# Column halves of w2, early norm weights and spread combining at the end of each layer's experts

## The chip, the cores and the metric

The kernel runs on one core of one Trainium2 chip. The metric is the time of one execution on the device in microseconds (us); several runs are taken and their median is compared. A profile of one execution gives the trace from which all rows below come. The engines are PE (matrix products), DVE and ACT (element-wise work), POOL, and SP, whose queue issues nearly all transfers.

## The reference

Two decoder layers and a closing norm over 512 tokens of width 1024, in float32. Layer 0 mixes tokens by forgetting attention, layer 1 by causal pooling over windows; behind each comes a mixture of 32 experts, of which every token takes two. Cut to what matters here:

```python
for i in range(DEPTH):
    h = modulate(rmsnorm(x, norm_mix_g[i]), sh_m, sc_m)
    y = fox_attention(...) if i % 2 == 0 else pool_mixer(...)
    x = x + gt_m * y
    h = modulate(rmsnorm(x, norm_ffn_g[i]), sh_f, sc_f)
    y = grouped_moe(h, ...)      # sum over chosen experts of w * (silu(h@w1) * (h@w3)) @ w2
    x = x + gt_f * y
return rmsnorm(x, norm_final_g)  # x * rsqrt(mean(x*x) + eps) * g
```

w1 and w3 are 1024 x 512 for each expert, w2 is 512 x 1024. All of them are read once from device memory: 32 experts, 6 MB each, in either layer.

## The kernel before, in words

The tokens lie in `xs` as four row blocks of 128 (t = 0 to 3), 1024 columns each. A layer's experts are worked off in 14 passes (`PASSES`); a pass takes one, two or four experts together. The last pass of each layer holds the four experts on places 8 to 11, each with at most 32 tokens, so that the products of the four stand side by side on 32 of 128 rows each (`parts`, with shares = 4).

**Weights.** `Stream` keeps a list of pieces of 1 MB in the order of use and 16 slots for them. `pump` issues the next piece on SP's queue whenever a slot is free; `done` frees a slot, with the last matmul that reads it. A pass of four experts has 8 pieces of w1, 8 of w3 and 8 of w2. A w2 piece (`expert_src`) is one half of the 512 inner rows with all 1024 columns: partition p holds the rows 4p to 4p+3, and half a of them (j = 2a, 2a+1) makes up a piece, 8 KB in one run for each partition. The pieces come in the order a = 0 of the four experts, then a = 1 of the four.

**A pass** (`step`, inside `experts`) multiplies the gathered tokens by w1 and w3 (`up`), gates them (`gated`), turns the result by transposes (`turn`) and multiplies by w2. In all passes but a layer's last, `down` fills two banks of 512 columns and the combining of a pass is done inside the next one. In a layer's last pass nothing follows, so it is written differently: `down_half` makes columns 0 to 511 first, `add_rows` spreads them over the four row blocks and adds them to `xs`, ACT takes the squares of that half for the norm (`half_length`), and then `down_half` makes columns 512 to 1023. Each half reads j = 0 to 3, so it needs all eight pieces; both are freed after the second half.

**After it** (`rows_step`) the second half is combined, square lengths are completed, and the norm's factor comes out. The order on PE, DVE, ACT and POOL is that of a hand-written string: `ORDER1` up to the bar for layer 0, `ORDER2` for layer 1. Its letters: K combines a row block on PE into a bank of tag c, T adds it to `xs` on DVE, Q takes the squares and R the root on ACT, N inverts on DVE. For layer 0, S is a small sum on PE, C scales `modC` on DVE by what S left, D scales the window matrix on DVE, and I multiplies by it on PE: with I the pooling layer begins. After `ORDER2` each row block of 1024 columns is multiplied by its factor and by the final norm weights in one DVE instruction (L1499) and sent out (L1500).

**Banks.** A tag of the PSUM pool has two banks. `add_rows` in the last pass and K use tag c alone for four row blocks, so that the third waits until the first has been added.

Of the kernel before, what the change touches and what calls it, by code (L numbers as in the profile page):

```python
# [24 lines left out]
D = 1024  # L25
T = 512
NT = 4
# [25 lines left out]
)  # L53
ORDER1 = (
# [9 lines left out]
)  # L64
ORDER2 = (
    "K0 K1 T0 Q0 R0 K2 T1 Q1 R1 N0 T2 K3 Q2 R2 N1 T3 Q3 R3 N2 N3 "
)


# [4 lines left out]
class Stream:  # L74
# [39 lines left out]
    def done(self, *keys):  # L114
        for key in keys:
            self.free[self.live.pop(key)[1]] += 1
        self.pump()
# [3 lines left out]
def kernel(  # L121
# [38 lines left out]
        stream.add(("wo", hf, a), attn_w_o[0].rearrange("(j p) n -> p j n", p=128)[  # L160
            :, 4 * a:4 * a + 4, 512 * hf:512 * hf + 512])

    def expert_src(w, l, k, a):

        static = k >= NE - STATIC
        e = k - (NE - STATIC) if static else order[l](k)
        v = w[l, e:e + 1] if static else w[l, ds(e, 1)]
        v = v.rearrange("o (p j) f -> p (o j) f", p=128)
        n = v.shape[1] // 2
        return v[:, n * a:n * a + n, :]  # L170

    def expert_items(l, i):

        for name, w in (("w1", exp_w1), ("w3", exp_w3), ("w2", exp_w2)):
            for a in range(2):
                for ab, k in enumerate(PASSES[i]):
                    stream.add((name, l, i, ab, a), partial(expert_src, w, l, k, a), lambda k=k: k >= NE - STATIC or l in order)

    order = {}

# [990 lines left out]
    def down_half(R, gT, gs, wt, hf, shares, done):  # L1171
        py = bank("y")
        for j in range(4):
            for r, ab in parts(shares):
                PE.matmul(py[r, :], gT[:, j, r], wt("w2", ab, j, hf), start=j == 0, stop=j == 3)  # L1175
        if hf:
            done("w2", 0)
            done("w2", 1)
        return weighted(R, gs, py, hf)

    def add_rows(PT, y, t, hf, tag="c"):
# [15 lines left out]
    def experts(R, aside):  # L1197
        l = R["l"]

        def weights(i):  # L1200
            def get(name, ab, j, hf):
                if hf is None:
                    return stream.get((name, l, i, ab, j // 4))[:, 512 * (j % 4):512 * (j % 4) + 512]
                at = 1024 * (j % 2) + 512 * hf
                return stream.get((name, l, i, ab, j // 2))[:, at:at + 512]

            def done(name, a):
                stream.done(*[(name, l, i, ab, a) for ab in range(len(PASSES[i]))])
            return get, done
# [22 lines left out]
        def step(i, xT, PT, gs, old, last):  # L1232

            w, done = weights(i)
            n = len(PASSES[i])
            p1, p3 = bank("h"), bank("h")
            if not last:
                Pn = choose(i + 1)
            if old:
                combine(old[0], old[1][0], 0, "cctt")  # L1240
            up(xT, w, "w1", p1, None if i else closing, n, done, (2, 6))
            if old:
                combine(old[0], old[1][1], 1, "ttyy")
            if not last:
                xg = gather(R, Pn)
            elif last == "layer":
                aside()
            up(xT, w, "w3", p3, None if i else closing, n, done, (2, 4, 6))
            g = gated(p1, p3)
            if not last:  # L1250
                xT = xgT()
                modulated(R, xg, xT)
            gT = turn(g)
            now = PT, gs
            if not last:
                PT, gs = chosen(i + 1, Pn)
            if last != "layer":
                return xT, PT, gs, (now[0], down(R, gT, now[1], w, n, done))
            y = down_half(R, gT, gs, w, 0, n, done)
            for t in range(NT):  # L1260
                add_rows(PT, y, t, 0)
                half_length(t, 0, mr("P16", [512], BF16))
                first_half(t)
            warm(AF.Sqrt, pre[:, NT - 1:])
            return PT, down_half(R, gT, gs, w, 1, n, done)

# [123 lines left out]
    def rows_step(PT, y, order):  # L1390
# [1 line left out]
        pa = {}  # L1392

        def K(t):
            ps = pa[t] = bank("c")
            PE.matmul(ps, PT[:, t, :], y[0], start=True, stop=False)
            PE.matmul(ps, PT[:, t, :], y[1], start=False, stop=True)

# [7 lines left out]
            root(t, pre[:, t:t + 1])  # L1406

        do = {"S": sums, "C": shift}
        for t in range(NT):
            for f in (K, T, Q, R):  # L1410
                do[f"{f.__name__}{t}"] = partial(f, t)
            do[f"N{t}"], do[f"D{t}"] = partial(inverse, t), partial(scaled, V, t)
            do[f"G{t}"] = partial(scaled, G, t)
# [75 lines left out]
    def gain():  # L1489
        last["fg"] = xgT().rearrange("p j t -> p (j t)")  # L1490
        G.dma_start(last["fg"], raw(norm_final_g, 0, [[0, 128], [1, D]]))

    end = experts(R, gain)
    with tc.manual_schedule(engines=BY_HAND):
        rows_step(*end, ORDER2)
    os = every([NT, 8, 128])
    for t in range(NT):
        o = os[:, t].rearrange("p j n -> p (j n)")
        V.scalar_tensor_tensor(o, xs[:, t, :], rstd[:, t:t + 1], last["fg"], op0=OP.mult, op1=OP.mult)  # L1499
        nc.sync.dma_start(out[0, 128 * t:128 * t + 128, :], o)  # L1500
    estack.close()


# [21 lines left out]
```

## Time and profile before

| | before |
|---|---|
| time, median of 3 runs | 1419.49 us (1413.96 to 1426.26) |
| the profiled execution's own time | 1410.96 us |
| its span, first to last instruction | 1409.4 us |
| PE busy | 1272.6 us, 90% of the span |
| DVE busy | 669.2 us, 47% |
| ACT busy | 384.6 us, 27% |
| mean granted TensorE clock | 0.967 of full |
| moved by transfers | 479.29 MB, 340 GB/s over the span |

A page of the profile cuts the span into 40 slices and gives in tenths how busy each engine was. In this one PE stands at 9 in most slices, the transfers too, with 410 to 421 GB/s in the stretches of experts; one slice between the two layers shows 74 GB/s, and the last slice 109 GB/s with PE at 4 tenths. A busy PE is not a PE at its peak, since its matmuls overlap; a wait shows in the timeline as idle time before an instruction, with what ended it.

### The profile page before, as it was taken

The numbers are of one execution on the slowest core, as the hardware profiler recorded it, in microseconds if no ns is written. First come the engines' busy times: TensorE is split into PE (matmuls) and PEld (weight loads), VectorE is DVE, ScalarE is ACT, GpSimd is POOL, SyncE is SP. The second block draws the span as 40 slices with busy tenths as digits, with TensorE's granted clock in tenths as the row PEclk, the third lists the DMA queues.
The fourth block names the chain that finished last, engine by engine and source line by source line (L and its number), as shares of the span: only waits on it lengthen the run. The fifth ranks groups of instructions, "written<-read, shape, count | busy, mean of one in ns | idle before, by whom it ended". The sixth has DMA issues, their size and how long they took to land. (4 is left out here: it accounts for less than half of the span.)

```text
span 1409.4 us, 18785 instructions
## 1 busy us (share of the span) xinstructions
PE 1272.6 (90%) x6688; PEld 665.7 (47%) x6689; DVE 669.2 (47%) x1306; ACT 384.6 (27%) x770; POOL 135.0 (10%) x90
## 2 busy tenths in 40 slices
PE   5789999888899699999999978899799999999984
PEld 2467777666443244444444425644244445444521
DVE  3787787885733233333334335743324334333423
ACT  3545555544421021111112104721021111111202
POOL 1513323425000000000000100100000000000000
PEclk9799999999999899999999997999999999999997
DMA  9654664756799999997999999289999998999992
GB/s 342 212 208 157 237 221 156 269 191 258 316 381 394 418 415 419 420 412 256 420 420 419 414 420 421 74 320 392 421 409 419 420 420 326 420 420 419 421 420 109
DMA packets 85000, 479.29 MB, mean 340 GB/s; under 512 B 12470, under 2 KB 25910, under 8 KB 29572
## 3 DMA queue, kind: packets, MB, share of 16 engines
q1 hardware_dynamic: 83776, 475.33, 84.2%
q10 hardware_dynamic: 496, 1.81, 0.4%
q8 instruction: 56, 0.92, 0.3%
q0 software_dynamic: 624, 0.84, 0.2%
q14 instruction: 48, 0.39, 0.1%
HBM read 475.55 MB, written 2.38 MB: 339 GB/s over the span
## 5 line engine op out<-in xcount | busy, mean ns | idle before, releaser
L1135 PE MATMUL h<-w,xgT 128*64 128x512 f32 (+2 forms) x2048 | 400.6, 595 | 1.3 <-ACT xgT L1070 0.6
L1135 PEld LDWEIGHTS h<-w,xgT 128*64 128x64 f32 (+2 forms) x2048 | 128.4, 130 | 237.4 <-issue 226.8
L1166 PE MATMUL y<-w,gT 128*64 128x512 f32 (+2 forms) x896 | 193.1, 596 | 16.7 <-DMA w<-in_exp_w_dram 9.9
L1187 DVE TENSOR_TENSOR xs<-xs,t 128x512 f32<-128x512 f32 x104 | 66.6, 682 | 144.0 <-PE t L1186 144.0
L1166 PEld LDWEIGHTS y<-w,gT 128*64 128x64 f32 (+2 forms) x896 | 60.4, 133 | 129.0 <-issue 99.8
L1156 DVE SCALAR_TENSOR_TENSOR y<-y,gs,gt 128x512 f32<-128x512 f32 x56 | 42.3, 755 | 162.4 <-PE y L1166 124.6
L701 POOL TENSOR_TENSOR wl<-w,wh 128x1024 fp32r<-128x1024 f32 x32 | 98.2, 3072 | 185.3 <-ACT wh L700 181.4
L1070 ACT ACTIVATE xgT<-t,modT 128x128 f32<-128x128 f32 x112 | 49.7, 458 | 206.7 <-PE t L1092 205.6
L1143 DVE TENSOR_TENSOR yl<-yl,h 128x512 f32<-128x512 f32 x28 | 19.3, 688 | 180.9 <-PE h L1135 161.6
L1126 ACT CAST yh<-y 128x512 fp32r<-128x512 f32 x56 | 32.9, 587 | 255.7 <-DVE y L1156 255.7
L301 DVE SCALAR_TENSOR_TENSOR lo<-w,cc,lo 128x2048 f32<-128x2048 f32 x28 | 82.1, 2931 | 0.4
L586 PE MATMUL c<-x,P 128*128 128x512 f32 x208 | 65.1, 436 | 9.0 <-DVE P L1101 9.0
L1141 ACT ACTIVATE yl<-h 128x512 f32<-128x512 f32 x28 | 16.8, 599 | 196.4 <-PE h L1135 196.4
L691 PE MATMUL h<-hi,wh 128*128 128x512 f32 x168 | 70.2, 418 | 0.0
L691 PE MATMUL h<-lo,wh 128*128 128x512 f32 x168 | 66.5, 396 | 0.0
L691 PE MATMUL h<-hi,wl 128*128 128x512 f32 x168 | 66.5, 396 | 0.0
L1075 DVE TENSOR_SCALAR yh<-c 128x512 f32<-128x512 f32 x26 | 18.0, 692 | 89.9 <-PE c L586 89.9
L586 PE MATMUL c<-lo,P 128*128 128x512 f16 x208 | 56.0, 393 | 0.0
L814 ACT ACTIVATE sb<-y,mx 128x128 f32<-128x128 f32 (+3 forms) x64 | 33.8, 528 | 75.7 <-DVE mx L813 73.4
L586 PEld LDWEIGHTS c<-x,P 128*128 128x128 f32 x208 | 40.4, 197 | 23.9 <-issue 12.0
L1127 DVE TENSOR_TENSOR yl<-y,yh 128x512 fp32r<-128x512 f32 x56 | 38.5, 688 | 21.1 <-ACT yh L1126 21.1
L1068 DVE TENSOR_SCALAR xgT<-t,modT 128x128 f32<-128x128 f32 x112 | 43.1, 406 | 9.2 <-ACT xgT L1070 8.5
(357 smaller groups left out, 1790.9 us busy)
## 6 DMA issues: line engine op xcount, KB each, us to landing
w<-in_exp_w_dram SPq DMA_DIRECT2D x384, 1024.0 KB, 17.9
w<-in_ada_w_dram SPq DMA_DIRECT2D x48, 1024.0 KB, 5.0
w<-in_attn_w_in_dram SPq DMA_DIRECT2D x12, 1024.0 KB, 7.4
w<-in_attn_w_o_dram SPq DMA_DIRECT2D x4, 1024.0 KB
xs<-in_x_dram SPq DMA_DIRECT2D x1, 2048.0 KB
out_dram<-x SPq DMA_DIRECT2D x4, 512.0 KB
gt<-row ACTq DMA_DIRECT2D x2, 512.0 KB
w<-in_pool_w_dram SPq DMA_DIRECT2D x1, 1024.0 KB
```

The lines of the kernel that those rows point to most:

```text
L301: V.scalar_tensor_tensor(ada_sum["s"], w, cc[:, j:j + 1], ada_sum["s"], op0=OP.mult, op1=OP.add)
L586: PE.matmul(pc[hf], P[part][:, t], R[("hi", "lo")[part]][:, t, 4 * hf:4 * hf + 4, :].rearrange("p j d -> p (j d)"), start=t == 0 and part ...
L691: PE.matmul(ps, a, b, start=first and n == 0, stop=last and n == 2)
L701: G.tensor_sub(lo, w, hi.bitcast(F32))
L814: S.activation(sb[:, h, :n], ps[:, :n], AF.Exp, bias=mx[:, h:h + 1], accum_out=ls[:, h:h + 1])
L1068: V.tensor_scalar(xT[:, j, :], ps, A, sh, op0=OP.mult, op1=OP.add)
L1070: S.activation(xT[:, j, :], ps, AF.Identity, scale=A, bias=sh)
L1127: V.tensor_sub(yl, y, yh.bitcast(F32))
L1135: PE.matmul(ps[r, :], xT[:, j, r], wt(name, ab, j, None), start=j == 0, stop=j == 7)
L1156: V.scalar_tensor_tensor(py, py, gs, R["gt"][:, 512 * hf:512 * hf + 512], op0=OP.mult, op1=OP.mult)
L1166: PE.matmul(py[hf][r, :], gT[:, j, r], wt("w2", ab, j, hf), start=j == 0, stop=j == 3)
L1187: V.tensor_add(xs[:, t, hs], xs[:, t, hs], ps)
```

## The change

Four things are edited; all else stays.

1. In a layer's last pass a w2 piece holds all 512 inner rows and one half of the columns (four runs of 2 KB for each partition instead of one of 8 KB). So `down_half` for half hf reads only the four pieces a = hf, and frees them when it is through. Size, number and order of the pieces stay.
2. Combining uses two tags: `add_rows` of the last pass c, c, t, t, and K c, c, h, h. In both orders K1 to K3 now stand right behind K0; in `ORDER1` that puts S behind K3, while C keeps its place on DVE.
3. Before the second half's products in layer 1, the first 512 columns of `xs` are multiplied by the final norm weights for all row blocks on DVE, into the output tile (`before_end`).
4. `ORDER2` ends with Z (invert, without N's second product), F (on ACT: the first half of the columns times the factor) and O (on DVE: the second half times factor and weights, 512 columns, and the transfer out).

```diff
 ORDER1 = (
-    "K0 S K1 T0 C Q0 K2 T1 R0 K3 Q1 N0 T2 R1 D0 Q2 T3 I10 ...
+    "K0 K1 K2 K3 S T0 C Q0 T1 R0 Q1 N0 T2 R1 D0 Q2 T3 I10 ...
 ORDER2 = (
-    "K0 K1 T0 Q0 R0 K2 T1 Q1 R1 N0 T2 K3 Q2 R2 N1 T3 Q3 R3 N2 N3 "
+    "K0 K1 K2 K3 T0 Q0 R0 T1 Q1 R1 Z0 T2 F0 O0 Q2 R2 Z1 T3 F1 O1 Q3 R3 Z2 F2 O2 Z3 F3 O3 "
...
-        return v[:, n * a:n * a + n, :]
+        return v[:, :, 512 * a:512 * a + 512] if columns else v[:, n * a:n * a + n, :]
...
-        if hf:
-            done("w2", 0)
-            done("w2", 1)
+        done("w2", hf)
...
-                at = 1024 * (j % 2) + 512 * hf
-                return stream.get((name, l, i, ab, j // 2))[:, at:at + 512]
+                a, at = (hf, 512 * j) if i == len(PASSES) - 1 else (j // 2, 1024 * (j % 2) + 512 * hf)
+                return stream.get((name, l, i, ab, a))[:, at:at + 512]
...
-                add_rows(PT, y, t, 0)
+                add_rows(PT, y, t, 0, "cctt"[t])
...
+            if l == 1:
+                before_end()
...
-            ps = pa[t] = bank("c")
+            ps = pa[t] = bank("cchh"[t])
...
+        def Z(t):
+            V.reciprocal(rstd[:, t:t + 1], rstd[:, t:t + 1])
+        def F(t):
+            o, r = last["os"][:, t], rstd[:, t:t + 1]
+            S.activation(o[:, :512], o[:, :512], AF.Copy, scale=r)
+        def O(t):
+            o, r = last["os"][:, t], rstd[:, t:t + 1]
+            V.scalar_tensor_tensor(o[:, 512:], xs[:, t, 512:], r, last["fg"][:, 512:], op0=OP.mult, op1=OP.mult)
+            nc.sync.dma_start(out[0, 128 * t:128 * t + 128, :], o)
...
+    def before_end():
+        for t in range(NT):
+            V.tensor_mul(last["os"][:, t, :512], xs[:, t, :512], last["fg"][:, :512])
...
-        V.scalar_tensor_tensor(o, xs[:, t, :], rstd[:, t:t + 1], last["fg"], op0=OP.mult, op1=OP.mult)
-        nc.sync.dma_start(out[0, 128 * t:128 * t + 128, :], o)
```

On PE, the end of layer 1 reads as follows in the kernel before, from the first product with w2 to the first row block combined. A row is a line of the code, what is written from what, and the signals waited for; each DMAHW signal is one piece of weights.

```order
L1175 MATMUL y<-w,gT 32x512 [waits DMAHW3_49,DVE_49]
L1175 MATMUL y<-w,gT 32x512 [waits DMAHW4_49]
L1175 MATMUL y<-w,gT 32x512 [waits DMAHW5_49]
L1175 MATMUL y<-w,gT 32x512 [waits DMAHW6_49]
L1175 MATMUL y<-w,gT 32x512 x4
L1175 MATMUL y<-w,gT 32x512 [waits DMAHW7_49]
L1175 MATMUL y<-w,gT 32x512 [waits DMAHW0_49]
L1175 MATMUL y<-w,gT 32x512 [waits DMAHW1_49]
L1175 MATMUL y<-w,gT 32x512 [waits DMAHW2_49]
L1185 MATMUL c<-yh,PT 128x512 [waits Activation_49]
```

The same place of the changed kernel:

```order
L1177 MATMUL y<-w,gT 32x512 [waits DMAHW6_49]
L1177 MATMUL y<-w,gT 32x512 x12
L1185 MATMUL c<-yh,PT 128x512 [waits Activation_49]
L1186 MATMUL c<-yl,PT 128x512 [waits DVE_49]
L1185 MATMUL t<-yh,PT 128x512
L1186 MATMUL t<-yl,PT 128x512
L1177 MATMUL y<-w,gT 32x512 [waits DMAHW7_49]
L1177 MATMUL y<-w,gT 32x512 [waits DMAHW0_49]
L1177 MATMUL y<-w,gT 32x512 [waits DMAHW1_49]
L1177 MATMUL y<-w,gT 32x512 [waits DMAHW2_49]
```

The four waits for the second four pieces stood ahead of the first half's combining and now stand behind it; 12 products follow the last of them, as 12 follow the fourth.

At the end of layer 0, on PE, the combining of the second half (yh, yl) and the sum S (from lo and ones_f); first before, then after:

```order
L1396 MATMUL c<-yh,PT 128x512 [waits Activation_49]
L1397 MATMUL c<-yl,PT 128x512 [waits DVE_49]
L1361 MATMUL t<-lo,ones_f 128x4 [waits PE_49,Pool_49]
L1396 MATMUL c<-yh,PT 128x512
L1396 MATMUL c<-yh,PT 128x512 [waits DVE_49]
```

```order
L1398 MATMUL c<-yh,PT 128x512
L1399 MATMUL c<-yl,PT 128x512
L1398 MATMUL h<-yh,PT 128x512 [waits PE_49]
L1399 MATMUL h<-yl,PT 128x512
L1363 MATMUL t<-lo,ones_f 128x4 [waits Pool_49]
```

S moved from behind the first row block to behind the fourth. On DVE, what waits for it (modC, which is C) stands second there in both kernels; the changed one reads:

```order
L1402 TENSOR_TENSOR xs<-xs,c 128x512 [waits PE_49]
L1367 TENSOR_TENSOR modC<-modC,t 128x8 [waits PE_49]
L1402 TENSOR_TENSOR xs<-xs,c 128x512
L376 RECIPROCAL rstd<-rstd 128x1 [waits Activation_49]
L377 TENSOR_SCALAR rstd_up<-rstd 128x1 [waits DVE_49]
L1402 TENSOR_TENSOR xs<-xs,h 128x512
L1380 TENSOR_SCALAR lo<-lo,rstd 128x4x16 [waits Pool_49]
```

So all of DVE's rows from the second row block on stand behind the moved S.

## Rows read from the trace of the kernel before

**Rows 1.** The page's first line: the span of the profiled execution.
```profile
span 1409.4 us, 18785 instructions
```

**Rows 2.** Stretches: from:to, length, busy of PE, PEld, DVE, ACT, POOL, clock, DMA share, GB/s.
```profile
884.00:895.00 11.00, 9.95 (x87) 8.56 (x86) 7.72 (x16) 9.53 (x19) 4.42 (x3) 1.00 0.04 15
...
1195.00:1366.00 171.00, 167.83 (x859) 75.01 (x857) 61.45 (x114) 25.68 (x49) 0.60 (x1) 1.00 1.01 420
```

**Rows 3.** Timeline, end of layer 1: start, duration, engine, line, operation; in brackets idle before.
```profile
1370.84 1.90 PE L1175 MATMUL y<-w,gT 128*32 128x512 f32 x10 [1.44 <-DMA w<-in_exp_w_dram]
...
1380.80 3.45 PE L1175 MATMUL y<-w,gT 128*32 128x512 f32 x10 [1.43 <-DMA w<-in_exp_w_dram]
...
1384.29 0.76 DVE L1156 SCALAR_TENSOR_TENSOR y<-y,gs,gt 128x512 f32<-128x512 f32 x1 [17.48 <-PE y L1175]
...
1389.79 4.11 PE L1175 MATMUL y<-w,gT 128*32 128x512 f32 x32
...
1393.97 0.76 DVE L1156 SCALAR_TENSOR_TENSOR y<-y,gs,gt 128x512 f32<-128x512 f32 x1 [2.39 <-PE y L1175]
...
1395.40 0.49 PE L1396 MATMUL c<-yh,PT 128*128 128x512 f32 x1 [1.51 <-ACT yh L1126]
```

**Rows 4.** Timeline, the same place at the end of layer 0.
```profile
848.85 3.62 PE L1175 MATMUL y<-w,gT 128*32 128x512 f32 x10 [1.46 <-DMA w<-in_exp_w_dram]
...
862.03 0.76 DVE L1156 SCALAR_TENSOR_TENSOR y<-y,gs,gt 128x512 f32<-128x512 f32 x1 [1.94 <-PE y L1175]
```

**Rows 5.** Timeline of PE in an earlier pass of four experts, layer 1.
```profile
1010.14 3.62 PE L1166 MATMUL y<-w,gT 128*32 128x512 f32 x26 [1.45 <-DMA w<-in_exp_w_dram]
```

**Rows 6.** Stretches around the last piece of layer 1, for the clock.
```profile
1368.00:1380.50 12.50, 6.09 (x18) 0.93 (x18) 0.00 (x0) 0.00 (x0) 0.00 (x0) 1.00 0.83 345
1380.60:1383.90 3.30, 3.10 (x10) 0.55 (x10) 0.00 (x0) 0.00 (x0) 0.00 (x0) 0.50 0.00 0
```

**Rows 7.** Stretches in which pieces with short runs moved, early in the kernel.
```profile
34.00:39.00 5.00, 1.96 (x8) 1.18 (x6) 4.67 (x8) 3.44 (x6) 2.30 (x1) 0.50 1.08 354
261.00:265.00 4.00, 4.00 (x27) 3.01 (x25) 2.56 (x6) 3.38 (x8) 0.17 (x2) 1.00 1.04 397
```

**Rows 8.** Timeline of SP's queue: what was issued for those stretches.
```profile
29.64 2.87 SPq L108 DMA_DIRECT2D w<-in_attn_w_in_dram  x3
...
256.46 2.74 SPq L108 DMA_DIRECT2D w<-in_attn_w_o_dram  x2
```

**Rows 9.** Timeline after the second half in layer 1.
```profile
1396.67 1.29 DVE L1400 TENSOR_TENSOR xs<-xs,c 128x512 f32<-128x512 f32 x2 [0.59 <-PE c L1397]
...
1397.45 0.63 ACT L365 ACTIVATE P<-xs 128x512 bf16<-128x512 f32 x1 [2.10 <-DVE xs L1400]
...
1398.20 0.29 ACT L371 ACTIVATE rstd<-ssq,pre 128x1 f32<-128x1 f32 x1
...
1399.39 1.28 DVE L1499 SCALAR_TENSOR_TENSOR x<-xs,rstd,xgT 128x1024 f32<-128x1024 f32 x1
...
1404.08 1.28 DVE L1499 SCALAR_TENSOR_TENSOR x<-xs,rstd,xgT 128x1024 f32<-128x1024 f32 x1
```

**Rows 10.** Groups of ACT by line and form: count, busy, mean ns, idle before.
```profile
L473 ACT ACTIVATE x<-xs,rstd_up 128x1024 fp32r<-128x1024 f32 x8 | 17.7, 2219 | 0.8 <-DVE rstd_up L375 0.8
L1141 ACT ACTIVATE yl<-h 128x512 f32<-128x512 f32 x28 | 16.8, 599 | 196.4 <-PE h L1135 196.4
```

**Rows 11.** Timeline, end of layer 0: S, C and the first window product.
```profile
864.52 0.28 PE L1361 MATMUL t<-lo,ones_f 128*128 128x4 f32 x2
...
865.33 0.15 DVE L1365 TENSOR_TENSOR modC<-modC,t 128x8 f32<-128x8 f32 x1
...
868.24 1.78 PE L1388 MATMUL y<-lo,xs 128*128 128x144 f32 x6 [0.70 <-DVE lo L1379]
```

**Rows 12.** Timeline of PE combining over two tags, a middle pass: first and last of eight.
```profile
1344.54 0.49 PE L1185 MATMUL c<-yh,PT 128*128 128x512 f32 x1
...
1346.75 0.40 PE L1186 MATMUL t<-yl,PT 128*128 128x512 f32 x1
```

More of the change, by code (lines that the diff above doesn't have):

```diff
@@ L161, in wo_item, with expert_src @@
             :, 4 * a:4 * a + 4, 512 * hf:512 * hf + 512])
-    def expert_src(w, l, k, a):
+    def expert_src(w, l, k, a, columns):
         static = k >= NE - STATIC
@@ L176, in expert_items @@
                 for ab, k in enumerate(PASSES[i]):
-                    stream.add((name, l, i, ab, a), partial(expert_src, w, l, k, a), lambda k=k: k >= NE - STATIC or l in order)
+                    stream.add((name, l, i, ab, a), partial(expert_src, w, l, k, a, name == "w2" and i == len(PASSES) - 1),
+                               lambda k=k: k >= NE - STATIC or l in order)
     order = {}
@@ L1408, in rows_step @@
         do = {"S": sums, "C": shift}
+        def Z(t):
[7 more added lines that the diff above has]
+            nc.sync.dma_start(out[0, 128 * t:128 * t + 128, :], o)
         for t in range(NT):
-            for f in (K, T, Q, R):
+            for f in (K, T, Q, R, Z, F, O):
                 do[f"{f.__name__}{t}"] = partial(f, t)
@@ L1491, in gain @@
         G.dma_start(last["fg"], raw(norm_final_g, 0, [[0, 128], [1, D]]))
+        last["os"] = every([NT, D])
+    def before_end():
+        for t in range(NT):
+            V.tensor_mul(last["os"][:, t, :512], xs[:, t, :512], last["fg"][:, :512])
     end = experts(R, gain)
@@ L1495 @@
         rows_step(*end, ORDER2)
-    os = every([NT, 8, 128])
-    for t in range(NT):
-        o = os[:, t].rearrange("p j n -> p (j n)")
-        V.scalar_tensor_tensor(o, xs[:, t, :], rstd[:, t:t + 1], last["fg"], op0=OP.mult, op1=OP.mult)
-        nc.sync.dma_start(out[0, 128 * t:128 * t + 128, :], o)
     estack.close()
```

2 rows, old and new, of the table ORDER1 are left out of this document.

## The prediction

> **What bounds the kernel now.** I began with the page's span [rows 1], then read a table of stretches [rows 2]: the reader is to see two regimes. Between the layers the transfers stand nearly still (15 GB/s at 884 to 895), because every slot is full and routing has not yet named the next experts; there the chain through PE, DVE and ACT sets the time. From 1195 to 1366 they run at 420 GB/s without a pause, one piece of 1.049 MB every 2.50 us, and PE is busy besides. Last I read the timeline where layer 1 closes [rows 3]. PE stands waiting for w2: the fourth piece releases it at 1370.84, the eighth only at 1380.80, since half 0 reads all eight. What follows the last piece is a chain: the rest of half 0 (3.45), its combining, half 1 from 1389.79 (4.11), at whose end DVE scales at 1393.97, and K0 at 1395.40. From the last piece to that scaling it is 13.17 us in layer 1, and 862.03 - 848.85 = 13.18 in layer 0 [rows 3, 4]. After K0, 14.0 us remain to the end of the span. These two stretches of 13.2 and the tail are what the change touches.
>
> **The pieces by column halves.** Half 0 now needs the first four pieces alone. Once the fourth is there, one product of that expert plus 12 of all four remain, 26 records in the trace's way of counting (each call shows as two). An earlier pass has this very pattern: 26 records behind a fourth piece took 3.62 us [rows 5]. So half 0 ends near 1370.84 + 3.6 = 1374.5 and its combining starts 1.5 later, the time PE stood idle between a half's last product and K0 (1.51 [rows 3]). Over two tags eight such matmuls take 1346.75 + 0.40 - 1344.54 = 2.6 us [rows 12], so PE is through at about 1378.6, ahead of the eighth piece. Half 1's first products are done as their pieces land, and the eighth releases again 26 records: scaling 3.65 us after the last piece instead of 13.2. That is 9.5 us in each layer if nothing else moves.
>
> **The price of runs of 2 KB.** No expert piece of before has them. The output weights of attention do; two such pieces were issued at 256.46 and moved, behind another, at 397 GB/s around 261 to 265 [rows 7, 8], against 420 with runs of 8 KB [rows 2]: 1.049/397 gives 2.64 us a piece, 0.14 more, 1.1 us for eight. The far bound is the input weights of attention, runs of 1 KB, at 354 GB/s [rows 7, 8]: 2.96 us, 3.7 for eight. The near bound is nothing. I take 1.1, the row with the same run length, so each layer keeps 8.4. The Trainium skill (DMA: Bandwidth & Descriptors, "Why small descriptors are slow") charges a fixed overhead of about three cycles for each packet, over 32-byte beats. By that, 67/64 against 259/256 is an estimate of 3.5%, 0.7 us for eight pieces; the trace shows 5.8%, and by the page the whole sum would be 0.8 us larger.
>
> **S behind K3 in layer 0.** Before, S ran at 864.52, and C at 865.33 found it done [rows 11]; K0 had started 1.43 after the scaling at 862.03, as 1395.40 stands to 1393.97 [rows 3, 4], so C came at K0 + 1.9. Now S comes after all eight matmuls, 2.6 us [rows 12], and takes 0.3: C can start at K0 + 2.9. Queued behind C on DVE are the second addition, the first inversion and the scaled window matrix, for which PE's first window product at 868.24 already waited 0.70 us [rows 11]. So that product comes up to 1.0 later, and nothing later if DVE has as long a pause of its own in between. I charge 0.7, since ACT's squares and root leave DVE some pause there. At the half clock the six matmuls between K0 and S, and S, take twice as long, 1.7 more. Layer 0 keeps 8.4 - 0.7 = 7.7.
>
> **Does layer 0's gain reach the end?** The slots were filled by 884, long before layer 1's first expert product, and the transfers then stood still until PE freed slots [rows 2]. Filling ends at the same clock time as before, some 1 us later at most, while PE needs it 8 us earlier: there is room. The restart is tied to routing and to PE, so it moves along; I count the gain in full. Freeing four slots earlier buys nothing itself, for the queue had work until 884 anyhow.
>
> **The tail.** From K0, DVE needed four additions (0.65), four products of 1.28 and small ones between them until 1404.08 + 1.28 = 1405.36 [rows 9]; this was the last chain. Now its products are half as wide, 0.64 each by the same row, which takes 2.6 us from DVE, while ACT needs 1.04 for a row block's squares and root (1397.45 to 1398.49 [rows 9]) and gets an F for each. F has no row; an ACT operation of that size takes 0.60, while one with a factor for each partition took 2.22 for 1024 columns, so 1.11 for 512, next to POOL reading the same tile [rows 10]. I take 0.60. Laid out in the order of the string with these durations, the first row block is ready 4.7 us after K0 and the last 8.6, against 5.3 (1399.39 + 1.28) and 10.0 before. The first gains 0.6 and the last 1.4; as the four transfers follow one another in one queue, I count 0.7 for the end. At 1.11 for F the last would be ready at 10.6, 0.6 later than before. `before_end` costs DVE 4 x 0.65: it lies between the end of combining at 1378.6 and half 1's scaling at 1385.6, 7 us in which DVE otherwise has only the first half's additions, 2.6, so it is covered; without that cover it would cost 2.6. The second tag for K removes waits of PE for additions, which DVE's own chain hides here; I count nothing.
>
> **The sum.** 8.4 + 7.7 + 0.7 = 16.8 us. The profiled execution's own time is 1410.96 (span 1409.4 [rows 1] and what lies around it), so it would be 1394.2. That execution was 8.5 below the median of the runs, and I take the difference from the median: 1419.49 - 16.8 = 1402.7 us.
>
> **Rivals.**
> *The clock falls again.* Behind the thin stretch from 1368 to 1380.5 (PE busy 6.1 of 12.5 at most) the granted clock was 0.50, 1.2 GHz of 2.4, and ten records took 3.45 instead of 1.90 [rows 3, 6]. If this happens at the last piece now, 26 records take some 7 us: 3.4 lost in each layer, and S costs 1.7 more: 16.8 - 6.8 - 1.7 = 8.3, 1411.2 us. For it: PE still waits for pieces. Against it: half 0's 26 records and the combining now lie in that stretch, and the row of 26 kept the pace of the full clock right behind such a wait [rows 5]. The Trainium skill (TensorE: Matmul & The Clock Gate, Part 1) says the gate follows how busy PE has lately been; the trace agrees with 0.50 after the thin stretch.
>
> *Layer 0's gain is lost.* If something fixed in time held layer 1's start, 8.4 + 0.7 = 9.1 would remain: 1410.4. Against it: the idle transfers [rows 2].
>
> *The short runs cost nothing.* 9.5 + 8.8 + 0.7 = 19.0: 1400.5.
>
> *The short runs cost much more.* 16 pieces lie on the path. The change turns into a loss when a piece takes 1.19 us more, 3.69 in all or 284 GB/s, and into one of over 1% at 228 GB/s, 2.1 us more: 1434 us. For it: runs of 1 KB already fall to 354. Against it: that is the lowest rate of a filled queue I found, and 2 KB showed 397 [rows 7].
>
> **Chances.** Forecast 0.58, clock 0.18, layer 0's gain lost 0.10, short runs free 0.10, short runs dear 0.04. A measurement of this kernel tells about 1%, 14.2 us, from no change; the forecast's gain is only 2.6 above that, and a half-clock stretch in one layer alone (3.4) would undo it, so I give 0.12 of its 0.58 to "within 1%". Faster by over 1%: 0.46 + 0.10 = 0.56. Within 1%: 0.12 + 0.18 + 0.10 = 0.40. Slower: 0.04. The range starts at 1392: the best the bounds allow (19.0), taken from the profiled execution's own 1410.96, since single runs of before lie that far below the median. It ends at 1412, which takes in the clock and the lost gain; what is outside is the dear short runs and an F at 1.11 on top of the clock.
>
> **What would show it.** In the trace after: at the end of either layer 26 records behind the fourth piece, combining on tags c and t, and 26 behind the eighth, about 3.6 us each at clock 1.00; from the last piece to half 1's scaling some 3.7 us instead of 13.2; last pieces 2.6 apart. In layer 0 C waits for PE about 1 us and the first window product comes about 0.7 later after K0. The idle stretch of the transfers between the layers is still there, some 8 us earlier at its end. F shows 0.6, and from K0 to the end it is 13.3 instead of 14.0. I am wrong if those 26 records take 7 us, if pieces are 3 us apart, or if PE meets a new wait for weights early in layer 1.

## The result and the profile after

| | before | after |
|---|---|---|
| median | 1419.74 us (1413.96 to 1426.26, 4 runs) | 1405.0 us (1402.49 to 1405.47, 4 runs) |
| the profiled execution's own time | 1410.96 us | 1404.75 us |
| its span | 1409.4 us | 1402.9 us |

The ratio is 0.9891 with the interval 0.9847 to 0.9936: 14.7 us less, just over 1%, where 1402.7 us had been predicted. The profiled executions lie only 6.2 us apart. Three lines of the page of after (its first line, one of part 1, one of part 2):

```profile
span 1402.9 us, 18788 instructions
...
PE 1267.1 (90%) x6688; PEld 667.9 (48%) x6689; DVE 668.8 (48%) x1306; ACT 386.9 (28%) x774; POOL 134.9 (10%) x90
...
DMA packets 91143, 479.27 MB, mean 342 GB/s; under 512 B 12470, under 2 KB 25910, under 8 KB 37764
```

The bytes are those of before to within 0.02 MB, and no engine's share of busy time moved by more than a point. Where the time went is in the timeline. The end of layer 1, which answers to [rows 3]:

```profile
1374.01 3.62 PE L1177 MATMUL y<-w,gT 128*32 128x512 f32 x26 [1.67 <-DMA w<-in_exp_w_dram]
...
1379.16 0.50 PE L1185 MATMUL c<-yh,PT 128*128 128x512 f32 x1 [1.53 <-ACT yh L1128]
...
1381.69 1.47 PE L1177 MATMUL y<-w,gT 128*32 128x512 f32 x6
1384.77 3.62 PE L1177 MATMUL y<-w,gT 128*32 128x512 f32 x26 [1.61 <-DMA w<-in_exp_w_dram]
...
1388.43 0.76 DVE L1158 SCALAR_TENSOR_TENSOR y<-y,gs,gt 128x512 f32<-128x512 f32 x1 [2.89 <-PE y L1177]
...
1389.86 0.50 PE L1398 MATMUL c<-yh,PT 128*128 128x512 f32 x1 [1.47 <-ACT yh L1128]
```

The reader sees both groups of 26 records, 3.62 us each. The first stands behind the fourth piece, the combining and the first products of half 1 are through before the eighth, and from the eighth piece to half 1's scaling it is 1388.43 - 1384.77 = 3.66 us, where it was 13.17. From the fourth piece to the eighth it is 10.76 us, 2.69 a piece; before it was (1380.80 - 1370.84) / 4 = 2.49 [rows 3]. Stretches of the same place (columns as in [rows 2]):

```profile
1366.00:1374.00 8.00, 3.63 (x15) 0.84 (x10) 1.38 (x2) 0.00 (x0) 0.00 (x0) 1.00 1.05 387
1374.00:1377.60 3.60, 3.59 (x26) 0.90 (x26) 0.00 (x0) 0.00 (x0) 0.00 (x0) 1.00 1.05 387
...
1384.80:1388.40 3.60, 3.59 (x26) 0.87 (x26) 0.75 (x2) 0.82 (x2) 0.00 (x0) 1.00 0.00 0
```

Runs of 2 KB move at 387 GB/s, and the granted clock stays at 1.00 behind the last piece, where [rows 6] had 0.50.

The end of layer 0, which answers to [rows 4] and [rows 11]:

```profile
843.21 5.32 PE L1177 MATMUL y<-w,gT 128*32 128x512 f32 x26 [1.12 <-DMA w<-in_exp_w_dram]
...
853.98 3.62 PE L1177 MATMUL y<-w,gT 128*32 128x512 f32 x26 [0.32 <-DMA w<-in_exp_w_dram]
...
857.64 0.76 DVE L1158 SCALAR_TENSOR_TENSOR y<-y,gs,gt 128x512 f32<-128x512 f32 x1 [2.43 <-PE y L1177]
...
859.07 0.50 PE L1398 MATMUL c<-yh,PT 128*128 128x512 f32 x1 [1.47 <-ACT yh L1128]
...
861.64 0.63 PE L1398 MATMUL h<-yh,PT 128*128 128x512 f32 x1
...
862.50 0.42 PE L1363 MATMUL t<-lo,ones_f 128*128 128x4 f32 x2
...
862.96 0.16 DVE L1367 TENSOR_TENSOR modC<-modC,t 128x8 f32<-128x8 f32 x1 [1.93 <-PE t L1363]
...
865.28 1.78 PE L1390 MATMUL y<-lo,xs 128*128 128x144 f32 x6 [2.36 <-DVE lo L1381]
```

From the eighth piece to the scaling it is again 3.66 us, against 13.18. C (at 862.96) now waits 1.93 us for S, and the first window product comes 865.28 - 859.07 = 6.21 us behind K0. Before it was 868.24 [rows 11] - 863.46 = 4.78; K0 stood there at

```profile
863.46 0.51 PE L1396 MATMUL c<-yh,PT 128*128 128x512 f32 x1 [1.53 <-ACT yh L1126]
```

The clock of these stretches after:

```profile
843.20:848.50 5.30, 5.29 (x26) 1.25 (x26) 0.00 (x0) 0.00 (x0) 0.00 (x0) 0.68 1.05 388
...
860.60:863.00 2.40, 2.32 (x7) 1.74 (x6) 0.47 (x2) 1.02 (x3) 0.00 (x0) 0.50 1.01 420
```

The half clock (granted 0.50) has not gone from layer 0. It stands in the first group of 26 (5.32 in place of 3.62), where it costs nothing, since PE still waits 0.32 us for the eighth piece; and it stands at K2, K3 and S, where it does.

The tail, which answers to [rows 9], from DVE, ACT and SP's queue:

```profile
1382.93 0.68 DVE L1511 TENSOR_TENSOR x<-xs,xgT 128x512 f32<-128x512 f32 x1
...
1393.80 0.71 ACT L1416 ACTIVATE x<-x,rstd 128x512 f32<-128x512 f32 x1
...
1394.53 4.05 SPq L1421 DMA_DIRECT2D out_dram<-x  x4
...
1396.90 1.32 ACT L1416 ACTIVATE x<-x,rstd 128x512 f32<-128x512 f32 x2
...
1397.23 0.75 DVE L1420 SCALAR_TENSOR_TENSOR x<-xs,rstd,xgT 128x512 f32<-128x512 f32 x1
```

F takes 0.66 to 0.71, O 0.75, the early products are through before half 1 is scaled, and from K0 to the end it is 1402.9 - 1389.86 = 13.0 us, where it was 14.0.

**Where the profiled spans differ.** Cutting both at the same instructions gives:

| stretch | before | after |
|---|---|---|
| start to the first w2 product of layer 0's last pass (A) | 836.60 | 841.03 |
| A to the first window product (I) | 31.64 | 24.25 |
| I to the first w2 product of layer 1's last pass (B) | 498.63 | 503.86 |
| B to the end | 42.53 | 33.76 |

The two stretches that the change touches lose 16.2 us, and the two that it doesn't touch gain 9.7. About half of this stands at one instruction. Between the third and the fourth pass of each layer (passes 2 and 3, counted from 0) the code calls `rest(R)`, whose loop takes care of tokens beyond an expert's slots; `with tc.If(top > 0)` skips it when there are none, as here. The condition's row on PE's queue, with its two durations (in ns, the smallest, their median, the largest; the largest is layer 0's), and who waited for it, in the kernel before and then after:

```profile
L1289 PEldq COMPARE_BRANCH  x2: 426/3317/6208, 479.9 to 1018.7; - x2
...
  DVE P L1101: 5.2, 2
```

```profile
L1291 PEldq COMPARE_BRANCH  x2: 5026/5568/6111, 484.2 to 1017.9; - x2
...
  DVE P L1103: 8.2, 2
```

In layer 1 the condition took 0.43 us before and 5.03 after. Behind it DVE chooses the next pass's rows (P) and PE gathers them; this gather's first rows in layer 1, before and after:

```profile
1021.88 1.82 PE L586 MATMUL c<-x,P 128*128 128x512 f32 x4 [2.26 <-DVE P L1101]
```

```profile
1024.00 2.04 PE L588 MATMUL c<-x,P 128*128 128x512 f32 x4 [5.31 <-DVE P L1103]
```

So there were two questions for the chip: which edit carries the gain, and whether the change itself makes this condition long.

### The profile page after: what moved, and what is told of

It reads as the page before. It is cut to its first block, busy times and chain, and to the rows that moved or that the text cites. A ratio compares the mean times of both kernels' runs of the same rounds, so it can differ in the third digit from the quotient of the medians.

```text
span 1402.9 us, 18788 instructions
## 1 busy us (share of the span) xinstructions
PE 1267.1 (90%) x6688; PEld 667.9 (48%) x6689; DVE 668.8 (48%) x1306; ACT 386.9 (28%) x774; POOL 134.9 (10%) x90
## 5 line engine op out<-in xcount | busy, mean ns | idle before, releaser
L1168 PE MATMUL y<-w,gT 128*64 128x512 f32 (+2 forms) x896 | 199.3, 622 | 16.5 <-DMA w<-in_exp_w_dram 9.7
L1143 ACT ACTIVATE yl<-h 128x512 f32<-128x512 f32 x28 | 16.8, 599 | 196.4 <-PE h L1137 196.4
L816 ACT ACTIVATE sb<-y,mx 128x128 f32<-128x128 f32 (+3 forms) x64 | 33.8, 528 | 75.7 <-DVE mx L815 73.2
L1185 PE MATMUL t<-yh,PT 128*128 128x512 f32 x108 | 46.4, 430 | 2.5 <-DVE xs L1187 2.5
```

The source lines that it names most:

```text
L816: S.activation(sb[:, h, :n], ps[:, :n], AF.Exp, bias=mx[:, h:h + 1], accum_out=ls[:, h:h + 1])
L1168: PE.matmul(py[hf][r, :], gT[:, j, r], wt("w2", ab, j, hf), start=j == 0, stop=j == 3)
```

## The experiments

All medians, in us, each beside runs of the kernel before on the same chip (1415 to 1419 us there):

| kernel | median (range, runs) | ratio to before |
|---|---|---|
| column halves alone | 1404.0 (1401.56 to 1408.47, 7) | 0.9903 (0.9866 to 0.9939) |
| after without column halves | 1417.32 (1409.99 to 1421.7, 12) | 0.9991 (0.9965 to 1.0017) |
| after, S behind K0 | 1403.89 (1398.64 to 1407.19, 6) | 0.9898 (0.9854 to 0.9942) |
| the same once more | 1399.83 (1395.06 to 1405.14, 6) | 0.9883 (0.9857 to 0.9910) |
| after once more | 1403.48 (1400.74 to 1406.28, 6) | 0.9888 (0.9848 to 0.9929) |
| before once more, for a second profile | 1416.14 (one run) | none taken |
| before, no condition | 1403.84 (1400.9 to 1407.03, 6) | 0.9901 (0.9869 to 0.9933) |
| after, no condition | 1384.26 (1382.48 to 1388.59, 6) | 0.9768 (0.9736 to 0.9799) |
| before, S behind K1 | 1418.81 (1415.42 to 1426.41, 12) | 1.0001 (0.9978 to 1.0023) |
| after, S behind K1 | 1403.09 (1396.2 to 1411.82, 6) | 0.9890 (0.9849 to 0.9932) |
| after, S twice | 1404.52 (1400.58 to 1405.52, 6) | 0.9904 (0.9881 to 0.9927) |
| next pass made ready ahead of the condition | 1382.73 (1380.63 to 1391.4, 6) | 0.9775 (0.9749 to 0.9801) |

And the stretches of their profiles in us, cut as above, from the starts in the timelines, with the time of layer 1's condition on PE's queue:

| kernel | start to A | A to I | I to B | B to end | condition |
|---|---|---|---|---|---|
| before | 836.60 | 31.64 | 498.63 | 42.53 | 0.43 |
| before once more | 838.35 | 31.71 | 502.13 | 42.41 | 5.40 |
| before, S behind K1 | 843.49 | 31.97 | 498.89 | 42.35 | 0.43 |
| after without column halves | 835.41 | 31.31 | 504.05 | 41.33 | 4.83 |
| column halves alone | 848.13 | 24.03 | 494.01 | 34.63 | 0.43 |
| after | 841.03 | 24.25 | 503.86 | 33.76 | 5.03 |
| after once more | 838.17 | 25.73 | 505.22 | 33.98 | 6.21 |
| after, S behind K1 | 842.92 | 23.95 | 502.97 | 33.76 | 5.39 |
| after, S behind K0 | 843.32 | 23.65 | 498.02 | 33.71 | 0.43 |
| the same once more | 836.27 | 24.19 | 499.28 | 33.76 | 0.41 |
| after, S twice | 842.16 | 24.78 | 503.31 | 33.75 | 6.03 |
| before, no condition | 833.21 | 31.09 | 495.69 | 42.11 | none |
| after, no condition | 830.68 | 24.26 | 493.80 | 33.36 | none |
| made ready ahead | 831.96 | 23.31 | 490.38 | 33.45 | 0.33 |

**Column halves alone, and all but them.** The first is the kernel before with edit 1, the second the changed kernel with edit 1 taken back. The core of the edit:

```diff
-        return v[:, n * a:n * a + n, :]
+        return v[:, :, 512 * a:512 * a + 512] if columns else v[:, n * a:n * a + n, :]
```

> The kernel before with the first edit alone: in a layer's last pass the w2 pieces hold column halves and each half frees its own four. Order strings, tags and closing norm are those of before. Theory A (the gain is the two stretches behind the last piece): from the last piece to the scaling of half 1 some 3.7 us instead of 13.2 in both layers, 8.4 us kept in each, none lost to S: 16.8 us, ratio 0.988. Theory B (layer 0's gain does not reach the end, as the trace of the changed kernel lets one suspect, where layer 1's second half starts only 1.6 us earlier in relation to layer 0's end): 8.4 us, ratio 0.994. If the tags and the norm carried the change, it would be near 1.

> The changed kernel with the first edit undone: w2 pieces by rows with 8 KB runs, both halves freed after the second. Tags, order strings and the early norm weights are those of the change. Theory A: the stretch behind the last piece is about 13 us again, less 1.1 for combining over two tags; the tail from K0 to the end is 13.0 as in the changed kernel instead of 14.0; S behind K3 costs 0.7 to 1.5 in layer 0. Sum: 1 + 1.1 + 1.1 - 1 = some 2 us faster than before, ratio 0.998 to 1.000. If it is faster by more than 5 us, the first edit is not what carries the gain.

Alone they give 0.9903; the first theory's 0.988 lies inside that interval and the second's 0.994 just outside. Without them nothing can be told from before. From A to I they take off 31.5 - 24.0 = 7.5 us, and from B to the end 42.4 - 34.6 = 7.8. What is left for the other edits shows in the last stretch: 42.4 to 41.3 without column halves, 34.6 to 33.8 with them, 0.8 to 1.1 us.

**S behind K0, and after once more.** One place in `ORDER1`:

```diff
-    "K0 K1 K2 K3 S T0 C Q0 T1 ...
+    "K0 S K1 K2 K3 T0 C Q0 T1 ...
```

> The changed kernel with S right behind K0 on PE in layer 0, as before the change; all else stays. In the changed kernel's trace DVE stands 1.93 us before C, waiting for S, and the first window product comes 6.21 us after K0's start, against 4.78 before. Theory A (the moved S costs layer 0 that 1.4): no such wait, the window product 4.8 us after K0, and the whole 1.4 us faster than the changed kernel, 0.1%, which the trace must show since times can't. Rival (the wait is covered by the pause before the inversion): the window product comes at 6 us all the same.

> The changed kernel once more, beside the other three on one chip, for a second trace of it. The first trace's span is only 6.5 us below that of before, while the stretches that the change touches gained 8.8 - 1.4 in layer 0, 8.4 in layer 1 and 1.0 in the tail, 16.8 in all; 4.4 us are missing ahead of layer 0's end, where nothing was changed, and some 5.7 between the layers' ends. Theory A (these 10 us differ from run to run and have no tie to the change): the median is 1419.7 - 16.8 = 1403, and in the second trace those two stretches take another length than in the first while the three touched ones are as in the first to 1 us. Theory B (layer 0's gain is taken back in layer 1): the stretch between the layers' ends is again 5 us longer than in the kernel before.

The timeline with S behind K0:

```profile
862.14 0.49 PE L1398 MATMUL c<-yh,PT 128*128 128x512 f32 x1 [1.47 <-ACT yh L1128]
...
863.20 0.42 PE L1363 MATMUL t<-lo,ones_f 128*128 128x4 f32 x2
...
866.97 0.97 PE L1390 MATMUL y<-lo,xs 128*128 128x144 f32 x6 [0.58 <-DVE lo L1381]
```

The first window product comes 4.83 us behind K0, as in the kernel before (4.78) and not as after (6.21): S behind K3 costs 1.4 us here. In the medians this doesn't show; on one chip they are 1403.89 and 1403.48. What the profiles did show was the condition, at 0.43 us with S early and about 6 with S late, which raised the suspicion that S's place makes it long. After once more has the median that theory A named (1403.48 for 1403). But its stretch I to B was long again (505.22, the sign of theory B), and A to I came out 1.5 us longer than in the first profile, so neither theory holds as it was written.

**The condition taken out of both kernels.**

```diff
-        rest(R)
```

> The kernel before without the call of rest(R), which leaves out the loop for the tokens beyond an expert's slots; these inputs never enter it, so only its outer condition and the reading of its bound go. In the profile of the kernel before, TensorE's queue spends 6.21 us on this condition in layer 0 and 0.43 us in layer 1. Theory 'the branch is on the path': the span falls by about 6.6 us, from 1409.4 to near 1403, the median from about 1419 to 1413, and the stretch from layer 1's first window product to its last pass's first w2 product stays at 498 us (498.63 before). Rival 'the branch is covered by the loads of the next weights': stretches and span stay within 2 us of the kernel before.

> The changed kernel without the call of rest(R) (the loop for the tokens beyond an expert's slots is left out, which these inputs never enter). In the profile of the changed kernel the condition takes TensorE's queue 6.11 us in layer 0 and 5.03 us in layer 1, where it was 0.43 us before. Theory 'the branch takes back a part of the gain': the stretch from layer 1's first window product to its last pass's first w2 product falls from 503.9-505.2 us to 498-499, as in the kernel without the call before the change; the span falls by about 11 us to near 1392, and the ratio between the two kernels without the call is near 0.986, against 0.989 with it. Rival 'the 5 us of the middle come from elsewhere': that stretch stays 5 us longer than in the other kernel without the call.

The condition is on the path, and costs more than its queue rows show. Taking it out saves 15.0 us in the kernel before (1418.79 to 1403.84), where the rows of both layers sum to 6.6 us in one profile and 11.4 in another. It saves some 19 us in the changed one (medians of two chips), where they sum to 11.1 and 12.3. I had expected 6.6 and 11. The difference between the kernels without it is 19.6 us (0.986, as expected), against 15 with it. I to B is 495.69 and 493.80 (498 to 499 expected), so the 5 us by which after's middle was longer are gone. The first gather behind the condition in layer 0, changed kernel with it and then without:

```profile
491.38 2.05 PE L588 MATMUL c<-x,P 128*128 128x512 f32 x4 [6.64 <-DVE P L1103]
```

```profile
481.82 1.09 PE L588 MATMUL c<-x,P 128*128 128x512 f32 x4
```

Without it four records take 1.09 us at a granted clock of 1.00 and nothing waits. With it PE has idled 6.64 us, and they take 2.05 at 0.50. PE's order differs too: without the condition the gather starts between the products of the combining ahead of it, which it does not do with the condition there. From pass 2's gather to pass 3's gather it is 68.4 to 71.3 us in layer 0 in the eleven profiles with the condition in its place and 58.5 to 59.2 without: 10.8 us by the means. In layer 1 it is 63.0 to 66.0 where the condition is short, 67.8 to 69.8 where it is long, and 60.9 to 61.2 without: by the means 3.7 and 7.4 us. 10.8 + 3.7 = 14.5 and 10.8 + 7.4 = 18.2 lie near the two measured differences, though these are of medians, over executions of either length. 19.6 - 15.6 (what the two touched stretches give in this pair) leaves 4 us in stretches with the same code, which I can't place.

**S behind K1, in both kernels.** The edit to the kernel before; in the changed one S moves from behind K3 to the same place.

```diff
-    "K0 S K1 T0 C Q0 K2 ...
+    "K0 K1 S T0 C Q0 K2 ...
```

> The kernel before with one letter of layer 0's end moved: S behind K1 in place of ahead of it; nothing else. Theory 'the place of S at layer 0's end decides how long the condition of layer 1 takes': the condition takes TensorE's queue about 5 us in layer 1 in place of 0.43, and the middle stretch of layer 1 grows from 498.6 to 503-505 us; the median is 0 to 5 us above that of the kernel before. Rival 'it was not S but the two tags of the combining, or the place of all four K': condition at 0.43 us, middle stretch 494 to 499 us, the median within 2 us.

> The changed kernel with S behind K1 in place of behind K3. With S behind K3 the condition of layer 1 took 5.03 and about 6.1 us in two profiles, with S behind K0 0.43 us. Theory 'S is late by the two products that go ahead of it': from half 1's scaling to layer 1's first window product near 6.9 us, between 6.26 (S behind K0) and 7.64 to 7.98 (behind K3). For the condition, theory 'one step from S behind K0 is enough': 5 to 6 us; rival 'only behind K3': 0.43 us. Median between 1403 and 1405 either way by the runs so far, in which S behind K0 and behind K3 could not be told apart.

In the kernel before the condition of layer 1 stayed at 0.43 us, in the changed one it was 5.39. The place of S alone doesn't decide it; the first theory of either expectation can't hold for both. The first window product was at 6.20 and 6.21 us behind the scaling, as if S stood early (6.21 to 6.26), so I expected too much (6.9): the cost of S comes with K2 and K3.

**The kernel before, and S behind K0, once more; S twice.** The last has one line twice, which moves every later instruction of PE by one:

```diff
         PE.matmul(mean["sum"][:, :4], ones_f, mean["m"][:, :, 127], start=True, stop=True)
+        PE.matmul(mean["sum"][:, :4], ones_f, mean["m"][:, :, 127], start=True, stop=True)
```

> The kernel before once more, for a second profile. Theory 'the length of layer 1's condition belongs to the kernel': TensorE's queue takes 6.0-6.2 us on it in layer 0 and 0.43 us in layer 1 again. Rival 'it belongs to the execution': 5 us in layer 1 this time. The ends of the layers (first w2 product of the last pass to the first window product: 31.1-32.0 us so far without column halves; in layer 1 to the last scaling: 26.8-27.1) should repeat in either case; the stretch ahead of layer 0's end, 833 to 848 us over ten profiles of the same code, should lie anywhere in between.

> The changed kernel with S behind K0 once more. Its condition in layer 1 took 0.43 us, that of the changed kernel 5.03 and 6.1, with the same instructions on TensorE in front of it but for S's place. Theory 'kernel': 0.43 us again, stretch from layer 1's first window product to its last pass near 498 us, and a median 4 us below the changed kernel's, near 1400 us. Rival 'execution': about 5 us this time and a median of 1403-1404 us like the changed kernel's.

> The changed kernel with S's small product issued twice (the second writes the same sums again). It moves every later instruction of TensorE one place on, as in the kernel before, whose condition in layer 1 was short. Theory 'the place in TensorE's program decides': the condition of layer 1 takes 0.43 us in place of 5-6, middle stretch near 498 in place of 503-505 us, median near 1400 us; the second product itself costs about 0.2 us. Rival 'not the place': condition 5-6 us, median 1403-1405 us.

The kernel before, a second time:

```profile
L1289 PEldq COMPARE_BRANCH  x2: 5397/5712/6028, 481.9 to 1020.9; - x2
...
  DVE P L1101: 8.5, 2
```

This settles one thing: the same program had the condition at 0.43 us in one execution and at 5.40 in another, so its length belongs to the execution, and after's 5.03 against before's 0.43 is no effect that the change must have. S behind K0 once more had it at 0.41 and a median of 1399.83 us, as its first theory asked, and moving the program by one instruction left it at 6.03. With S ahead of K1 it was short in five of six profiles, with S later in one of six; chance alone would split twelve profiles as unevenly about once in twelve times, so that S's place shifts the odds is not shown.

The traces show what goes with the length. One transfer queue of the page, q8, is of the kind "instruction" and moves 16 KB at a time (56 packets, 0.92 MB in the page of before). Its line in the kernel before from 1012 to 1018.71 us, ahead of the short condition:

```profile
q8 instruction: 1, 0.02, 1.0%
```

In the second execution no transfer of q8 begins from 992 us to the condition at 1020.89 (all queues of that stretch), and one begins within the 5.40 us of the condition:

```profile
q1 hardware_dynamic: 1657, 12.08, 100.9%
q14 instruction: 1, 0.01, 0.1%
```

```profile
q8 instruction: 1, 0.02, 1.2%
```

It is so in all twelve profiles with the condition. All 18 long rows, of both layers, have a q8 transfer that starts 2.35 to 3.76 us into the row, and the row ends 2.5 us after that start (2.47 to 2.51); the last one before it lies 17 us or more ahead. The six short rows have had theirs 5.0 to 12.9 us before they begin, and none starts inside. So by these times the long condition is a wait for this transfer. What lets it come early in one execution and late in another of the same program stays open.

**The next pass made ready ahead of the condition.** Without the condition the kernel lacks a part that other inputs need. So the last run keeps it (with S behind K0), and moves what stood behind it: choosing, gathering and scaling the rows of pass 3 are done beside pass 2's products, as in every other pass. The loop takes its weights into another buffer, since both of the first kind are now in use.

```diff
-                xT, PT, gs, old = step(i, xT, PT, gs, old, None if i + 1 < HALF else "half")
+                xT, PT, gs, old = step(i, xT, PT, gs, old, None)
...
-            Pn = choose(HALF)
-            xT = xgT()
-            modulated(R, gather(R, Pn), xT)
-            PT, gs = chosen(HALF, Pn)
...
-                            w = xgT().rearrange("p j t -> p (j t)")[:, :512]
+                            w = u2("yl", 2, [512])
```

> The changed kernel with S behind K0, and with the choosing, gathering and scaling of the rows of pass 3 put ahead of rest(R)'s condition, beside the products of pass 2, where they stood behind it; the overflow loop takes another buffer for its weights (these inputs never enter it). Nothing is left out. Without the condition the two kernels were 15 and 19 us faster, 10.8 of it in layer 0, of which TensorE's queue shows only 6.2. Theory 'the rest is the chain of choosing and gathering that can't begin before the condition is through': the condition stays at 6 us in layer 0 and 0.4 to 6 in layer 1, but 4 to 5 us are saved in layer 0 and 3 to 4 in layer 1; median 1392 to 1396 us, against 1399.8 and 1403.9 of the kernel without this edit. Rival 'the next pass waits for its weights': the chain is gone from behind the condition, w1's first product begins no earlier by more than 2 us, median 1398 to 1404 us.

1382.73 us, ratio 0.9775 (0.9749 to 0.9801): the fastest kernel of this study that leaves nothing out, 2.25% under the kernel before. These inputs never enter the loop, so no run shows it with its new buffer. Its page's first line, and PE around the condition in layer 0:

```profile
span 1379.1 us, 18806 instructions
```

```profile
482.16 0.40 PE L1186 MATMUL y<-yl,PT 128*128 128x512 f32 x1
488.70 9.19 PE L1137 MATMUL h<-w,xgT 128*64 128x512 f32 x32 [6.14 <-PEq L1287]
```

And the same place after (S behind K3):

```profile
484.35 0.39 PE L1186 MATMUL y<-yl,PT 128*128 128x512 f32 x1
491.38 2.05 PE L588 MATMUL c<-x,P 128*128 128x512 f32 x4 [6.64 <-DVE P L1103]
...
499.23 2.36 PE L1137 MATMUL h<-w,xgT 128*64 128x512 f32 x9
```

From the last product of the combining to the first of w1 it is now 6.54 us (6.1 of it the condition itself) in place of 14.88; in layer 1 it is 2.34, against 10.32 and 10.33 in the two profiles of S behind K0, all three with a short condition. I had expected 4 to 5 and 3 to 4 us and got 8.3 and 8.0: the expectation had counted the cost beyond the queue's time (10.8 - 6.2) and not the whole chain from 491.38 to 499.23, 7.85 us, which runs slowly behind PE's pause. A part of that slowness stays: w1's 32 records in layer 0 now stand behind the pause and take 9.19 us at a granted clock of 0.77, where after's took 7.09 at 1.00.

## Why the prediction was right

**What bounds the ends of the layers: right.** The fourth piece in place of the eighth releases half 0, and 26 records stand behind the last piece; 3.66 us from it to the scaling in both layers, 3.65 predicted.

**The price of runs of 2 KB: too low.** 2.69 us a piece, not 2.64; against 2.49 that is 0.20, so 1.6 us for eight in place of 1.1. The rate was 387 GB/s, between the 397 and 354 that I had as rows [rows 7]; the row taken is a stretch of 4 us, and why it moved faster isn't shown. The gain of the column halves comes out at 7.5 to 7.8 a layer, not 8.4. The Trainium skill (DMA: Bandwidth & Descriptors, "Why small descriptors are slow") led to an estimate of 3.5% for this; the trace shows 8%, so here the measurement decides.

**S behind K3: too low, because of the clock.** 1.4 us by the timelines, not 0.7. In the two profiles of after the granted clock fell to 0.50 at K2, K3 and S, and the first window product came 6.21 and 6.55 us behind K0. In after without the condition it stayed at 1.00 there (columns as in [rows 2]), and the product came 5.09 us behind K0:

```profile
849.85 0.50 PE L1397 MATMUL c<-yh,PT 128*128 128x512 f32 x1 [1.47 <-ACT yh L1128]
...
854.94 0.97 PE L1389 MATMUL y<-lo,xs 128*128 128x144 f32 x6 [2.36 <-DVE lo L1380]
```

```profile
849.85:854.95 5.10, 2.51 (x11) 1.83 (x11) 3.65 (x10) 2.52 (x8) 0.00 (x0) 1.00 1.01 419
```

So at the full clock S's place costs 0.3 us, less than the 0.7 charged, and the half clock adds 1.1 to 1.5. The prediction had a price for that (six products and S at the half clock, 1.7) but left it to the rival. Over all profiles with column halves, A to I is 24.8 us in the mean of four with S behind K3 and 23.8 in four with S behind K0, so 1.0 is nearer as a mean.

**The tail: near.** 13.0 us from K0 to the end for 13.3 predicted, 1.0 gained for 0.7. F takes 0.66 to 0.71 for an assumed 0.60, far from the bound of 1.11, and O 0.75 for an assumed 0.64.

**`before_end` is covered: right.** It runs from 1382.93 into the wait for half 1's 26 records, and DVE still idles 2.89 us before the scaling at 1388.43.

**Layer 0's gain reaches the end: right.** The transfers still pause between the layers. First after, in three stretches, then two of before:

```profile
890.00:896.00 6.00, 5.58 (x46) 4.75 (x45) 5.18 (x21) 4.77 (x11) 0.00 (x0) 1.00 0.03 10
...
902.00:908.00 6.00, 4.73 (x20) 2.31 (x20) 5.16 (x33) 2.53 (x4) 0.00 (x0) 0.50 0.00 0
908.00:914.00 6.00, 5.13 (x27) 2.91 (x26) 5.00 (x14) 2.48 (x6) 0.00 (x0) 0.99 0.14 49
```

```profile
908.00:914.00 6.00, 4.98 (x27) 2.67 (x26) 5.24 (x18) 1.56 (x4) 0.00 (x0) 0.87 0.00 0
914.00:920.00 6.00, 5.49 (x32) 2.30 (x33) 4.54 (x21) 2.40 (x6) 0.00 (x0) 1.00 0.25 90
```

From 896 to 902 both kernels move about 170 GB/s; behind that the transfers start again between 908 and 914 after, and between 914 and 920 before. I had said 8 us earlier; in this pair the first window product is only 3.0 earlier (865.28 against 868.24), as layer 0's last pass began 4.4 later. The slots were filled later by as much (350 GB/s from 884 to 890 after, 25 before), which left room enough. No new wait for weights came up in the passes of layer 1: between I and B PE's waits for weights sum to 4.8 us before and 4.1 after. Where the condition was short, I to B is 494.0 to 499.3 us with column halves and 498.6 and 498.9 without.

**The sum.** With S where the change puts it, A to I falls from 31.5 (mean of five without column halves) to 24.8, B to the end from 42.35 (four kernels with the old tail and no column halves) to 33.7: 6.7 + 8.6 = 15.3 us, against 16.8. The medians give 14.7 and, beside runs on another chip, 15.8. So 1.5 of the 2.3 us between 1402.7 and 1405.0 are the terms above; the rest is less than the runs tell.

**The base.** Taking the sum from the median was the right choice and the profiled execution the wrong one for a forecast: 1410.96 - 16.8 = 1394.2 would have missed by over 10 us. That execution of before was among the quickest, with the condition of layer 1 short. Why runs of before spread over some 15 us and those of after, of which there are fewer, over 3 to 6 isn't settled; the condition's two lengths are worth 4 us of it.

**What the prediction left out.** It has neither a term nor a rival for the condition, whose length in layer 1 differs by some 4 us between executions. The terms of the sum were near; that the total came out near with this one uncounted is in part luck. If all of before's runs were short there and all of after's long, some 4 us of the gain would be lost, and the runs don't tell how often each is.

**The rivals.** The half clock at the end did come in layer 0, at places that cost 1 us and not 8; in layer 1 of this profile it stayed away. Layer 0's gain was not lost. Short runs are neither free nor dear.

## What to carry to other kernels

Where a half of a product waits for all pieces of a weight, cut the pieces so that the first half needs only some of them: work moves from behind the last transfer to beside it, at the price of shorter runs, which should be taken from a row of a filled queue with that run length (here even such a row, of 4 us, was 2.5% too fast). Before measuring a change of 1%, cut several profiles of the same kernel at the same instructions; in this kernel, what varied in stretches that nothing touched was as large as the change. In this unrolled program the next pass's choosing and gathering didn't begin until a condition in its middle was through: where a kernel has one, have the next step's inputs ready ahead of it.

## What the runs showed of the hardware

A condition that is never entered cost 15 to 19 us over its two places together. On DVE, ACT, POOL and SP its row takes 0.05 to 0.07 us; on PE's queue 6.0 to 6.3 in layer 0 in every profile, and in layer 1 either 0.33 to 0.43 or 4.8 to 6.2; one program had 0.43 in one execution and 5.40 in another. PE's pace behind it was halved too: four records of the gather took 2.05 us at a granted clock of 0.50, and 1.09 at 1.00 where no condition stood ahead.

The Trainium skill (Runtime: NRT & Kernel Launch, "Instruction fetch mechanics") says that a taken branch whose target isn't in the window already fetched has to wait for a fetch. The traces agree: each long row ends 2.5 us after a 16 KB transfer of the instruction queue q8 has started inside it, and no short row has one inside. That q8 is PE's is inferred from these times; no view names the engine.
